# Float32 one-hots of the gate table laid out token by token

## The chip, the cores and the metric

The kernel runs on one core of a Trainium2 chip. The core has a matrix engine (TensorE, PE in the profile, with its weight loads shown apart as PEld), a vector engine (VectorE, DVE), a scalar engine (ScalarE, ACT), GpSimd (POOL) and a queue engine (SyncE, SP). They run side by side, each through its own list of instructions in order, and wait for each other by semaphores. The metric is the time of the program on the device in microseconds (us); smaller is better.

## The reference, cut to what matters

The program is one residual layer: two token mixers in parallel (RWKV-7 and S5), then PEER, a mixer over 128 x 128 = 16384 one-neuron experts, then a norm. What the change touches is PEER:

```python
sv, si = lax.top_k(s, PEER_TOPK)                       # 16 best of 128 keys, for both key halves
cv, ci = lax.top_k(cand.reshape(...), PEER_TOPK)       # 16 best of the 256 pairs
i1 = jnp.take_along_axis(si[:, :, 0], ci // PEER_TOPK, axis=-1)
i2 = jnp.take_along_axis(si[:, :, 1], ci % PEER_TOPK, axis=-1)
gate = jax.nn.softmax(cv, axis=-1)
hid = jax.nn.gelu(jnp.einsum('td,thkd->thk', xt, table_u[e]))    # e = i1 * 128 + i2
return jnp.einsum('thk,thkd->td', gate * hid, table_v[e])
```

Each of the 1024 tokens chooses 8 heads x 16 = 128 experts with a gate each. Everything is float32.

## The kernel before

The tokens stand in eight blocks of 128. Three blocks gather the rows of their experts from memory. The other five ("dense", 640 tokens) compute the scores of all 16384 experts with matmuls and weight them with a gate table that is zero wherever a token did not choose the expert. This table, `gd` in device memory, is made before the dense part by `gate_table`, one block of 128 tokens after the other.

For a token, the table is a 128 x 128 matrix, first key by second key. It is a product of two one-hot matrices with the 128 choices of the token on the partitions: `a` has a 1 at the second key of each choice, `b` has the gate at its first key. So a token needs one 128x128x128 float32 matmul `gm`, which the machine runs as two weight loads and two matmul instructions. The tokens go through in groups of four (TG = 4); 640 tokens are 160 groups and 1280 gm instructions. In a group:

- VectorE compares a constant `iotaM` with the keys, in bfloat16, for `aq` and for `bq` (in the profile `oaq` and `ohq`), all [128, 128 keys, 4 tokens], the four tokens innermost
- ScalarE (for a few groups VectorE) copies `aq` to float32 as `a` (`oha`)
- GpSimd, or VectorE where the planner found it free earlier, multiplies `bq` by the gates `gT` into float32 `b` (`ohb`)
- TensorE runs the four matmuls with `a[:, :, t]` as weights and `b[:, :, t]` as the moving side: 128 values that lie four floats (16 bytes) apart, since the tokens are interleaved
- ScalarE copies the four results from PSUM into `stg`, which holds 32 tokens, token innermost; so each token's 128 values are written 32 floats (128 bytes) apart. After eight groups a 2 MB transfer writes `stg` to `gd`

The buffers: three of `oha`, three of `ohb`, two of `ohq`, one of `oaq`, two PSUM banks of `gm`, two of `stg`.

The order of the instructions is not that of the code. A planner (class `Weave`) runs fourteen streams of the program as threads: the RWKV state, the top-k retrieval, the table, the gathers, the dense part and others. Each stream hands in operations; the planner holds estimated costs per engine (`cost`, by element counts alone, blind to strides), keeps a clock of every engine and of every buffer, and emits at each step the ready operation with the highest bonus on the engine that is free first. `nc.copy` and `nc.either` offer an operation to two engines, and it takes the one that would end first by its estimate. What it emits is then the fixed order of each engine. A buffer that is handed out again makes its next writer wait for the last reader. While the table is built, the last RWKV steps, the retrieval of the later blocks and, towards the end, the first dense scores `S` are woven between the groups. All operations go through one helper line, so the profile names them by tile. The dense stream with its gate loads `G` begins after the last table block.

Of the kernel before, what the change touches and what calls it, by code (L numbers as in the profile page):

```python
# [19 lines left out]
F32 = mybir.dt.float32  # L20
F32R = mybir.dt.float32r
BF = mybir.dt.bfloat16
# [3 lines left out]
OP = mybir.AluOpType  # L26
# [17 lines left out]
TG = 4  # L44
# [7 lines left out]
GW = 2  # L52
HG = 0
PB = 2
OA = 4
BV = 0
BDP = "none"
TREE = 1
# [316 lines left out]
class Kern:  # L375
# [1147 lines left out]
    def gate_table(self, blk, e, g, pool):  # L1523


        nc, v = self.nc, self.nc.vector
        p = self.ps("gp", [128, 3, 128], 1, self.psg)
        for i, src in enumerate((e[:, :, 0], e[:, :, 1], g)):
            x = pool.tile([128, 128], F32, name=self.nm("slc"), tag="slc", bufs=1)
            nc.copy(x.rearrange("p (h k) -> p h k", h=8), src)  # L1530
            nc.tensor.transpose(p[:, i], x, self.ident)
        iT = pool.tile([128, 2, 128], BF, name=self.nm("iT"), tag="iT", bufs=2)
        gT = pool.tile([128, 128], F32, name=self.nm("gT"), tag="gT", bufs=2)
        nc.copy(iT, p[:, 0:2])
        nc.copy(gT, p[:, 2])
        for t32 in range(4):
            stg = pool.tile([128, 128, 32], F32, name=self.nm("stg"), tag="stg", bufs=2)
            for t16 in range(32 // TG):
                t0 = 32 * t32 + TG * t16
                shp = [128, 128, TG]  # L1540
                bc = lambda x: x[:, None, t0:t0 + TG].to_broadcast(shp)
                a = pool.tile(shp, F32, name=self.nm("oha"), tag="oha", bufs=3)
                bq = pool.tile(shp, BF, name=self.nm("ohq"), tag="ohq", bufs=2)
                b = pool.tile(shp, F32, name=self.nm("ohb"), tag="ohb", bufs=3)
                if t16 % 4 < OA:
                    aq = pool.tile(shp, BF, name=self.nm("oaq"), tag="oaq", bufs=1)
                    v.tensor_tensor(aq, self.iotaM, bc(iT[:, 1]), op=OP.is_equal)
                    nc.copy(a, aq)
                else:
                    v.tensor_tensor(a, self.iotaM, bc(iT[:, 1]), op=OP.is_equal)  # L1550
                v.tensor_tensor(bq, self.iotaM, bc(iT[:, 0]), op=OP.is_equal)
                nc.either("tensor_tensor", b, bq, bc(gT), op=OP.mult)
                for t4 in range(TG // 4):
                    ps = self.ps("gm", [128, 4, 128], GMB, self.psg)
                    for i in range(4):
                        t = 4 * t4 + i
                        nc.tensor.matmul(ps[:, i], a[:, :, t], b[:, :, t], start=True, stop=True)
                    o = TG * t16 + 4 * t4
                    nc.copy(stg[:, :, o:o + 4].rearrange("p i t -> p t i"), ps)
            nc.sync.dma_start(self.gd[4 * DB.index(blk) + t32], stg)  # L1560
        self.tabled += 1
# [546 lines left out]
```

## Time and profile before

| | |
|---|---|
| time, median of 3 runs | 3720.68 us (3716.93 to 3731.84) |
| profiled execution, its own time | 3725.95 us |
| span in it, from first to last instruction | 3723.9 us |
| mean granted TensorE clock | 0.947 of full |
| busy: PE, PEld, DVE, ACT, POOL | 93%, 80%, 74%, 36%, 32% |
| the table stage, first to last `gm` | about 1274 to 1694 us |

Busy shares are means over a long program of unlike stages; what one stage is worth is read from rows of that stage. An instruction's duration counts from its start to its last result, so instructions that follow each other on one engine overlap: how fast an engine gets through them is read from the starts, or from the busy time of a stretch divided by the count.

### The profile page before, as it was taken

Reading aid. Unit: us, or ns where it says so; the run is one execution under the profiler, and the core shown is the slowest. Engines: PE = TensorE matmul, PEld = TensorE weight load, DVE = VectorE, ACT = ScalarE, POOL = GpSimd, SP = SyncE. Lnnn points to the kernel's source line nnn. Section 1 sums busy time; section 2 is a strip of 40 time slices with the busy share of each in tenths; the row PEclk is TensorE's granted clock in tenths of the full one; section 3 lists DMA queues with packets and bytes.
Section 4 is the critical chain, followed back from the end, with each engine's and each line's share of the span. In section 5 each row is a group of like instructions: output and inputs, shape, how many; then the busy total and the mean of one; then the engine's idle time right before and its main releaser. Section 6 shows DMA issues by size and latency. Waiting matters only on the chain.

```text
span 3723.9 us, 59743 instructions
## 1 busy us (share of the span) xinstructions
PE 3446.2 (93%) x22415; PEld 2975.6 (80%) x22415; DVE 2757.2 (74%) x6150; ACT 1346.6 (36%) x2905; POOL 1191.9 (32%) x1137
## 2 busy tenths in 40 slices
PE   7989999999888999998998889988999999999997
PEld 7777687767666888897787778887989998888986
DVE  7555413546999967654788978888888888888888
ACT  4332323333232466663233323333333333333333
POOL 3653323532443344432222222122222222222221
PEclk9998999998889899899999899998999999999998
DMA  5641223355577422257888799877898988898886
GB/s 205 215 152 54 88 96 119 129 195 187 168 260 236 166 100 92 98 191 255 312 318 317 246 327 334 304 269 276 304 323 303 323 316 308 306 322 290 304 298 228
DMA packets 359953, 869.11 MB, mean 233 GB/s; under 512 B 28960, under 2 KB 175520, under 8 KB 307952
## 3 DMA queue, kind: packets, MB, share of 16 engines
q1 hardware_dynamic: 303792, 461.01, 36.8%
q0 software_dynamic: 55296, 402.68, 29.4%
q8 instruction: 176, 2.88, 0.3%
q10 hardware_dynamic: 576, 1.61, 0.1%
q14 instruction: 113, 0.93, 0.1%
HBM read 759.16 MB, written 104.86 MB: 232 GB/s over the span
## 4 chain that ended last, share of the span: by engine, by line
PE 48%; DVE 19%; issue 15%; DMA 10%; POOL 5%; ACT 2%; SPq 1%; POOLq 0%; DVEq 0%; ACTq 0%
PE S L171 11%; PE acc L171 10%; PE gm L171 9%; PE mm L171 7%; POOL row L171 5%; DMA G<-gd 3%; PE tps L171 3%; PE rs L171 2%; PE gl L171 2%; PE rw L171 2%; DVE gacc L171 2%; PE pp L171 1%; DMA row<-in_uv_dram,ei 1%; DMA w<-in_wout_dram 1%; DVE ti L171 1%
## 5 line engine op out<-in xcount | busy, mean ns | idle before, releaser
L171 POOL DMA_INDIRECT row<-in_uv_dram,ei x384 | 519.0, 1352 | 1499.2 <-DVE gacc L171 1253.4
L171 PE MATMUL S<-dx,uh 128*128 128x320 f32 x4096 | 790.4, 314 | 8.5 <-ACT w L171 6.1
L171 PEld LDWEIGHTS S<-dx,uh 128*128 128x128 f32 x4096 | 656.9, 190 | 27.9 <-ACT w L171 9.5
L171 PE MATMUL acc<-vh,wh 128*128 128x512 f32 x1280 | 504.3, 402 | 64.1 <-DVE acc L171 61.7
L171 DVE SCALAR_TENSOR_TENSOR gacc<-row,hid,gacc 128x1024 f32<-128x1024 f32 x384 | 491.2, 1279 | 71.7 <-ACT hid L171 71.1
L171 PE MATMUL acc<-vl,wh 128*128 128x512 f32 x1280 | 511.2, 399 | 11.2 <-DVE vl L171 11.0
L171 PE MATMUL acc<-vh,wl 128*128 128x512 f32 x1280 | 509.4, 398 | 0.1
L171 PE MATMUL S<-dx,ul 128*128 128x320 f32 x2048 | 478.4, 314 | 13.0 <-DVE ul L171 13.0
L171 DVE CUSTOM_DVE_ANT_0 row<-row,gx 128x1024 f32<-128x1024 f32 x384 | 468.3, 1220 | 18.1 <-DMA row<-in_uv_dram,ei 18.0
L171 PEld LDWEIGHTS S<-dx,ul 128*128 128x128 f32 x2048 | 346.8, 190 | 17.9 <-DVE ul L171 15.9
L171 PE MATMUL gm<-ohb,oha 128*128 128x128 f32 x1280 | 343.1, 430 | 5.5 <-ACT oha L171 5.0
L171 PEld LDWEIGHTS acc<-vh,wh 128*128 128x128 f32 x1280 | 244.0, 191 | 128.0 <-DVE acc L171 67.2
L171 PEld LDWEIGHTS gm<-ohb,oha 128*128 128x128 f32 x1280 | 311.3, 329 | 14.3 <-ACT oha L171 5.1
L171 PEld LDWEIGHTS acc<-vl,wh 128*128 128x128 f32 x1280 | 246.2, 192 | 61.4 <-DVE vl L171 15.5
L171 PEld LDWEIGHTS acc<-vh,wl 128*128 128x128 f32 x1280 | 245.7, 192 | 54.7 <-issue 1.7
L171 ACT ACTIVATE hid<-hid 128x1 f32<-128x1 f32 x384 | 77.2, 201 | 564.2 <-DVE hid L171 563.3
L171 ACT ACTIVATE vh<-vr 128x512 fp32r<-128x512 f32 x256 | 160.3, 627 | 284.2 <-PE acc L171 166.3
L171 DVE TENSOR_TENSOR acc<-acc,acc 128x512 f32<-128x512 f32 x320 | 213.0, 682 | 6.9 <-PE acc L171 6.4
L171 ACT ACTIVATE stg<-gm 128x512 f32<-128x512 f32 x160 | 172.5, 1079 | 119.2 <-PE gm L171 116.5
L171 POOL TENSOR_TENSOR ohb<-ohq,gT 128x512 f32<-128x512 bf16 x135 | 146.0, 1082 | 212.8 <-DVE ohq L171 116.1
L171 DVE TENSOR_TENSOR vl<-vr,vh 128x512 fp32r<-128x512 f32 x255 | 174.3, 685 | 52.4 <-ACT vh L171 52.1
L171 DVE TENSOR_TENSOR w<-w,G 128x640 f32<-128x640 f32 x128 | 105.1, 821 | 144.7 <-DMA G<-gd 114.3
(443 smaller groups left out, 6241.8 us busy)
## 6 DMA issues: line engine op xcount, KB each, us to landing
ur<-in_ut_dram SPq DMA_DIRECT2D x128, 512.0 KB, 6.5
vr<-in_uv_dram SPq DMA_DIRECT2D x256, 256.0 KB, 6.4
wf<-wsd SPq DMA_DIRECT2D x120, 512.0 KB, 5.5
gd<-stg SPq DMA_DIRECT2D x20, 2048.0 KB, 6.6
G<-gd SPq DMA_DIRECT2D x31, 1280.0 KB, 16.6
wsd<-sw SPq DMA_DIRECT2D x40, 512.0 KB, 3.4
wr<-in_wc_dram SPq DMA_DIRECT2D x30, 512.0 KB, 4.7
wr<-in_wg_dram SPq DMA_DIRECT2D x32, 256.0 KB, 3.3
```

The lines of the kernel that those rows point to most:

```text
L171: op.alts = [(e, self.cost(e, n, outs, ins), lambda f=f, a=a, k=k: f(*a, **k)) for e, n, f, a, k in alts]
```

## The change

`a` and `b` become [128, 4 tokens, 128 keys], a token's 128 values side by side. The copy and the gate product write them through a turned view (`turn`), in the old order of elements, so that consecutive elements go to places 128 floats (512 bytes) apart. The matmuls read `a[:, t]` and `b[:, t]`, 128 adjacent floats. The comparisons and their results in bfloat16 stay as they were. `oaq` gets two buffers instead of one, and the branch on `OA`, which was always taken, goes.

```diff
-OA = 4
...
-                a = pool.tile(shp, F32, name=self.nm("oha"), tag="oha", bufs=3)
+                a, b = (pool.tile([128, TG, 128], F32, name=self.nm("oh" + x), tag="oh" + x, bufs=3) for x in "ab")
+                turn = lambda x: x.rearrange("p t m -> p m t")
                 bq = pool.tile(shp, BF, name=self.nm("ohq"), tag="ohq", bufs=2)
-                b = pool.tile(shp, F32, name=self.nm("ohb"), tag="ohb", bufs=3)
-                if t16 % 4 < OA:
-                    aq = pool.tile(shp, BF, name=self.nm("oaq"), tag="oaq", bufs=1)
-                    v.tensor_tensor(aq, self.iotaM, bc(iT[:, 1]), op=OP.is_equal)
-                    nc.copy(a, aq)
-                else:
-                    v.tensor_tensor(a, self.iotaM, bc(iT[:, 1]), op=OP.is_equal)
+                aq = pool.tile(shp, BF, name=self.nm("oaq"), tag="oaq", bufs=2)
+                v.tensor_tensor(aq, self.iotaM, bc(iT[:, 1]), op=OP.is_equal)
+                nc.copy(turn(a), aq)
                 v.tensor_tensor(bq, self.iotaM, bc(iT[:, 0]), op=OP.is_equal)
-                nc.either("tensor_tensor", b, bq, bc(gT), op=OP.mult)
+                nc.either("tensor_tensor", turn(b), bq, bc(gT), op=OP.mult)
...
-                        nc.tensor.matmul(ps[:, i], a[:, :, t], b[:, :, t], start=True, stop=True)
+                        nc.tensor.matmul(ps[:, i], a[:, t], b[:, t], start=True, stop=True)
```

The order of the instructions moves inside the table stage alone; ahead of it and behind it the engines' lists are as they were. The second buffer of `oaq` is what moves it: the planner's estimates do not see the strides. The count of copies on ScalarE goes from 156 to 158 of 160 (VectorE 4 to 2), and of gate products on GpSimd from 135 to 126 (VectorE 25 to 34).

ScalarE, near the start of the table stage, before. `stg` is a group's evacuation, `oha` a group's copy; the numbers of `gm` and `oha` grow with the groups, and the group of oha2654 is evacuated from gm2658, that of oha2659 from gm2664.

```order
L171 ACTIVATE oha2654_13897<-oaq2657_13905 128x512
L171 ACTIVATE stg2594_13714<-gm2653_13896 128x4x128
L171 ACTIVATE oha2659_13916<-oaq2662_13925 128x512
L171 ACTIVATE stg2594_13714<-gm2658_13915 128x4x128
L171 ACTIVATE oha2666_13936<-oaq2669_13946 128x512
L171 ACTIVATE Z2635_13839<-rx2637_13881 128x256
L171 ACTIVATE stg2594_13714<-gm2664_13934 128x4x128
```

The same place after the change; here the group of oha2660 is evacuated from gm2664.

```order
L170 ACTIVATE oha2660_13918<-oaq2663_13921 128x128x4
L170 ACTIVATE stg2594_13714<-gm2653_13893 128x4x128
L170 ACTIVATE oha2666_13937<-oaq2669_13940 128x128x4
L170 ACTIVATE stg2594_13714<-gm2658_13917 128x4x128
L170 ACTIVATE oha2672_13959<-oaq2675_13962 128x128x4
L170 ACTIVATE stg2594_13714<-gm2664_13935 128x4x128
```

Before, a copy stands one evacuation ahead of its own group's evacuation; after, two, so the copies run one group further ahead.

VectorE, some groups later, before. `ohq` and `oaq` are the two comparisons of a group, the rest is retrieval and RWKV work.

```order
L171 TENSOR_TENSOR ohq_13983<-iotaM,iT_13712 128x512
L171 MAX tv_13122<-t_13921 128x8
L171 TENSOR_TENSOR oaq_13991<-iotaM,iT_13712 128x512
L171 MAX_INDEX ti_13123<-tv_13122,t_13921 128x8
L171 MAX tv_13120<-sc_13611 128x8
L171 TENSOR_TENSOR ohq_14005<-iotaM,iT_13712 128x512
L171 MAX_INDEX ti_13121<-tv_13120,sc_13611 128x8
L171 TENSOR_TENSOR oaq_14015<-iotaM,iT_13712 128x512
```

The same place after the change.

```order
L170 TENSOR_TENSOR oaq_13980<-iotaM,iT_13712 128x512
L170 TENSOR_TENSOR ohq_13979<-iotaM,iT_13712 128x512
L170 MAX_INDEX ti_13123<-tv_13122,sc_13553 128x8
L170 MATCH_REPLACE t_13912<-tv_13122,sc_13553 128x128
L170 TENSOR_TENSOR abm_13991<-pb_12577,cst 128x256
L170 TENSOR_TENSOR oaq_14008<-iotaM,iT_13712 128x512
L170 TENSOR_TENSOR ohq_14007<-iotaM,iT_13712 128x512
```

The two comparisons of a group now stand together, `oaq` first, with the other work behind the pair and not between.

## Rows read from the trace of the kernel before

**Rows 1.** The page: span, and busy time of each engine

```profile
span 3723.9 us, 59743 instructions
PE 3446.2 (93%) x22415; PEld 2975.6 (80%) x22415; DVE 2757.2 (74%) x6150; ACT 1346.6 (36%) x2905; POOL 1191.9 (32%) x1137
```

**Rows 2.** Windows: busy us (instructions) by engine, granted clock, DMA share, GB/s

```profile
core 0: us, PE busy (x) PEld busy (x) DVE busy (x) ACT busy (x) POOL busy (x), PEclk, DMA share, GB/s
1274.00:1694.00 420.00, 406.11 (x2405) 372.73 (x2405) 272.64 (x741) 270.51 (x412) 182.77 (x161) 0.92 0.31 117
1280.00:1580.00 300.00, 291.06 (x1890) 259.99 (x1889) 211.66 (x612) 189.26 (x302) 135.40 (x121) 0.91 0.23 95
1580.00:1694.00 114.00, 109.31 (x491) 107.59 (x491) 54.98 (x116) 77.41 (x105) 43.80 (x38) 0.96 0.52 179
1720.00:1760.00 40.00, 27.66 (x140) 23.41 (x141) 23.86 (x35) 8.21 (x20) 5.22 (x4) 0.83 0.76 264
```

**Rows 3.** Windows of the evacuation `stg` alone: ScalarE's busy us (count)

```profile
1280.00:1580.00 300.00, 117.30 (x111) 0.91 0.23 95
1580.00:1694.00 114.00, 52.07 (x49) 0.96 0.52 179
```

**Rows 4.** The chain of waits: start us, us, what

```profile
1586.85 23.66 PE gm L171 x96
1610.51 0.11 PE gp L171
...
1693.88 1.15 ACT stg L171
1695.04 7.66 DMA gd<-stg
1702.76 8.27 DMA G<-gd
```

**Rows 5.** Instructions on `gm`: duration ns min/median/max, first and last start

```profile
L171 PEld LDWEIGHTS gm<-ohb,oha x1280: 307/332/335, 1274.0 to 1693.2; 128*128 128x128 f32 x183
L171 PE MATMUL gm<-ohb,oha x1280: 388/416/604, 1274.0 to 1693.4; 128*128 128x128 f32 x183
```

**Rows 6.** The same view of RWKV's float32 128x128 matmuls with adjacent values

```profile
L171 PEld LDWEIGHTS rm<-lo,lora x192: 186/191/337, 386.7 to 1416.8; 128*128 128x128 f32 x192
L171 PE MATMUL rm<-lo,lora x192: 270/275/422, 386.7 to 1416.9; 128*128 128x128 f32 x192
```

**Rows 7.** Groups of instructions of the table stage: busy us, mean ns, idle before

```profile
L171 PE MATMUL gm<-ohb,oha 128*128 128x128 f32 x1280 | 343.1, 430 | 5.5 <-ACT oha L171 5.0 <-issue 0.5
L171 ACT ACTIVATE stg<-gm 128x512 f32<-128x512 f32 x160 | 172.5, 1079 | 119.2 <-PE gm L171 116.5 <-DMA gd<-stg 2.5
L171 POOL TENSOR_TENSOR ohb<-ohq,gT 128x512 f32<-128x512 bf16 x134 | 145.0, 1082 | 200.1 <-DVE ohq L171 116.1 <-PE gm L171 51.2 <-DVE rtrg L171 10.5
L171 ACT ACTIVATE oha<-oaq 128x512 f32<-128x512 bf16 x155 | 98.2, 633 | 15.8 <-DVE oaq L171 15.8
L171 DVE TENSOR_TENSOR oaq<-iotaM,iT 128x512 bf16<-128x512 bf16 x159 | 93.1, 585 | 121.3 <-ACT oha L171 112.7 <-ACT iT L171 7.9
L171 DVE TENSOR_TENSOR ohb<-ohq,gT 128x512 f32<-128x512 bf16 x25 | 18.2, 727 | 4.2 <-PE gm L171 3.5
```

**Rows 8.** Groups of whole program: PSUM copies to adjacent places, and one to places apart

```profile
L171 ACT ACTIVATE sc<-tp 128x512 f32<-128x512 f32 x24 | 14.3, 597 | 25.2 <-PE tp L171 25.2
L171 DVE TENSOR_TENSOR h<-mm,h 128x512 f32<-128x512 f32 x12 | 8.1, 685 | 6.6 <-PE mm L171 6.6
L171 DVE COPY yT<-tps 128x512 f32<-128x512 f32 x8 | 8.6, 1152 | 17.5 <-PE tps L171 17.5
```

**Rows 9.** Timeline of ScalarE: start us, us, instruction, idle before

```profile
1448.36 1.04 ACT L171 ACTIVATE stg<-gm 128x512 f32<-128x512 f32 x1 [1.21 <-PE gm L171]
1449.20 0.63 ACT L171 ACTIVATE oha<-oaq 128x512 f32<-128x512 bf16 x1
```

## The prediction, made before the changed kernel had run

> **What bounds the kernel now.** I read the page first: PE is busy 93% of a span of 3723.9 us [rows 1], so where a stage has PE waiting for nothing, time spent by PE is time of the program. Then the windows around the only instructions that the change alters, the table stage from 1274 to 1694 us: PE is busy 406.1 of 420 us, VectorE 272.6, ScalarE 270.5, GpSimd 182.8 [rows 2]. So this stage is TensorE's. Third, the groups: the gm matmuls take 343.1 us of PE and were kept waiting 5.5 us, while ScalarE's evacuation `stg` waited 116.5 us for gm, and VectorE's `oaq` 112.7 us for the copy `oha` that frees its single buffer [rows 7]: the other engines queue up behind gm. Last, the chain of waits: it runs through gm, once through 96 of them without a break, and from the last evacuation over the last write of `gd` straight into the first gate load of the dense part [rows 4]. What the stage loses in length, the program loses, since behind it the instructions and their order are the same.
>
> **What the change removes.** In the unbroken run 96 instructions take 23.66 us, 246 ns each [rows 4]. Their neighbour `gp`, a float32 128x128 instruction on adjacent values, takes 0.11 us of the chain [rows 4]. The durations say the same: gm's loads and matmuls have medians of 332 and 416 ns, the adjacent `rm` of the same shape 191 and 275 [rows 5, 6], 141 ns less on either side. With gm at 110 ns, PE is relieved of 1280 x 136 ns = 174 us, and its 406 us in the stage become 232. Its bound there is gone, and what is late next decides.
>
> A rule of the Trainium skill bears on this: "SBUF — State Buffer", section "Door 1: The DMA port swizzle", holds that 4 float32 values is as far as one can stride for free, since a line has 16 bytes. By that figure the interleaved reads would cost nothing and the change would leave the time at 3721. The rows differ: the loads at that stride take 332 against 191 ns [rows 5, 6]. The measurement decides.
>
> **What it adds.** The writers now step 512 bytes from element to element. The trace has no such write, but two with steps: `stg` writes 128 bytes apart and takes 1079 ns, where a ScalarE copy from PSUM of the same size to adjacent places takes 597 [rows 7, 8]; VectorE's `yT`, 32 bytes apart, takes 1152, where a VectorE operation from PSUM to adjacent places takes 685 [rows 8]. So a stepped float32 write costs 470 to 480 ns more on both engines, about twice the time per element. From this:
>
> ScalarE: 158 copies x 0.48 = +76 us. The bounds of this price are 0 (if a copy from SBUF hides it) and about twice 0.48 (if 512 bytes are worse than 128); I take 0.48, the value of the row nearest in engine and size.
>
> VectorE: 34 products at 727 + 470 = 1197 ns are 40.7 us against 18.2 before, +22 us; the two copies that leave it give back 1. Bounds 0 and +45.
>
> GpSimd: no stepped write of it is in the trace. Its product takes 1082 ns for 512 elements [rows 7], slower than the stepped write of either other engine by element minus its fixed part, so the step may vanish in it. Bounds: 0, and three times its duration. I take between 0 and 0.5 us each, at most 126 x 1.58 = 199 us in place of 145, and GpSimd at 183 + 54 = 237 us: off the path either way.
>
> The second `oaq` buffer takes away VectorE's wait for the copy of the group just before; the wait for the one before that stays, and the copies stand one group further ahead in ScalarE's list. This hides under PE before and matters only now, since ScalarE's evacuation no longer finds gm unfinished.
>
> **The sum.** By groups: the first part, with RWKV and retrieval woven in, has 111 groups in 300 us, 2.70 us each; the second 49 in 114, 2.33 us each [rows 2, 3]. In the first part ScalarE needs 189.3/111 = 1.71 us per group now, and 1.71 + 0.47 = 2.18 after. That counts records that start behind idle time. Where its list is full, the next one starts 0.84 us after a `stg` of 1.04 [rows 9], so a full list would get through the two stepped writes in 1.7 and some 0.2 of the rest, 1.9. VectorE needs 211.7/111 = 1.91 us, and 2.04 after. PE needs 2.62 - 8 x 0.136 = 1.53. ScalarE and VectorE are then equals at about 2.0 to 2.1, they wait for each other, and PE before reached 97% alone; I take 2.2 us per group. In the second part VectorE has little else (55.0/49 = 1.12), ScalarE needs 1.58 + 0.47 = 2.05, or 1.9 with a full list: I take 2.0. So 111 x 0.50 + 49 x 0.33 = 56 + 16 = 72 us less. The stage would take about 348 us. The changes of block, where index transposes, copies and comparisons must run through before the next gm, cost a few us each and stay.
>
> Against the profiled execution's own time of 3725.95 (2 us over its span) that is 3654. The median of the runs lies 5.3 us lower at 3720.68, which gives **3649**.
>
> **Rivals.**
>
> *The stepped copy is free on ScalarE.* For it: its source is SBUF and half as wide, unlike `stg`'s. Against: VectorE and ScalarE pay the same in the two rows there are, which points to the write. Then VectorE binds in the first part at about 2.1 and ScalarE in the second at 1.65: 111 x 0.60 + 49 x 0.68 = 100 us less, 3621.
>
> *The gain is eaten.* If the copy's step costs twice `stg`'s (+0.95 us), ScalarE needs 1.71 + 0.94 = 2.65 us in the first part and 2.5 in the second, with overlap perhaps 0.2 less: the stage stays within 20 us of 420, the time at 3705 to 3735, say 3718. For it: 512 bytes is four times as far; against: 32 and 128 bytes cost the same.
>
> *TensorE's clock falls.* In the stage the granted clock is 0.92 with PE busy 97%; behind it, where PE is busy 27.7 of 40 us (69%), it is 0.83 [rows 2], a mix of the levels 1.2 and 2.4 GHz. After the change PE would have 232 of 348 us, 67%, so a clock near 0.83 is likely, and 232 x 0.92/0.83 = 257 us still fits. At the lower level throughout, an adjacent matmul needs up to 422 - 275 = 147 ns more [rows 6], 1280 x 0.257 = 329 us with gm alone, 392 with the other 63 as they are: the stage would shrink by some 27 us and the time be 3694. The Trainium skill, "TensorE: Matmul & The Clock Gate", section "A second HAM failure mode: psum-queue depth-cycling", describes this kind of stage: short idle times between groups make the clock fall back again and again. The 0.83 of rows 2 agrees in kind.
>
> *GpSimd's stepped product is slow.* If it handles such writes one by one at 4 us a product, 126 x 4.0 + 38 of other work = 542 us, and the stage takes 120 us longer: 3843. It decides from (420 - 38)/126 = 3.0 us a product, three times today's duration, at which all its work fills the old stage. Nothing in the trace excludes it, but neither engine that shows such writes pays more than twice.
>
> *The stride is not what makes gm slow.* Then nothing changes on PE: 3721. Rows 5 and 6 have the same shape and type and differ in the stride alone, so this is small.
>
> **Chances.** Forecast 0.60 (3620 to 3680 is its own range); free copy 0.14; gain eaten 0.09; clock 0.07; GpSimd 0.06; stride not the cause 0.04. About 0.5%, 19 us, is what a measurement of this kernel can tell from no change. Faster by more: the forecast, the free copy, most of the clock case and a little of the eaten gain, 0.82. Within: most of the eaten gain, stride and a rest of the others, 0.11. Slower: GpSimd and a piece of the eaten gain, 0.07. The range 3605 to 3705 takes in the free copy with some room and the clock case, and leaves GpSimd and the eaten gain out.
>
> **What would show it.** gm's loads near 190 ns and matmuls near 275. `oha` on ScalarE near 1.1 us; if it is 0.63, the first rival. `ohb` on GpSimd below 1.6 us; if over 3, the fourth. The stage from first to last gm near 350 us, with PE at about two thirds, ScalarE at over 90%, and `stg` no longer waiting for gm but ScalarE waited for by gm and `oaq`. Behind the stage the lengths should be as before to within some us; if the dense part grows by what the stage loses, the argument that the stage's length passes through is wrong.

## The result, and the profile after

The change makes the kernel faster: 3671.61 us (median of 4 runs, 3657.96 to 3678.38) against 3722.39 of the kernel before in the same comparison, a ratio of 0.9851 with a 95% interval of 0.9824 to 0.9878. Run again later beside other kernels it gave 3669.61 us and 0.9864 (0.9824 to 0.9905). That is 50 to 55 us. The forecast was 3649, 72 less than before, with a range of 3605 to 3705: the direction holds and TensorE's bound is gone as argued; the size was set too high.

The profiled execution has a span of 3666.8 us, 57.1 less. The page first: TensorE's busy share fell, though the kernel got faster, and that of VectorE and ScalarE rose; rows 1 had 93%, 74% and 36%.

```profile
span 3666.8 us, 59750 instructions
PE 3317.5 (90%) x22415; PEld 2841.2 (77%) x22415; DVE 2807.3 (77%) x6159; ACT 1398.3 (38%) x2906; POOL 1205.8 (33%) x1127
```

The instructions on `gm` and its makers after the change (duration in ns, minimum, median, maximum; first and last start). They answer to rows 5: gm's load and matmul now have the durations of the adjacent `rm` of rows 6, and the last gm starts at 1631 instead of 1693. The stepped copy takes 1122 ns, the stepped product 1120 on GpSimd and 1068 on VectorE (medians).

```profile
L170 PEld LDWEIGHTS gm<-ohb,oha x1280: 186/192/338, 1274.9 to 1631.1; 128*128 128x128 f32 x183
L170 PE MATMUL gm<-ohb,oha x1280: 272/275/582, 1274.9 to 1631.2; 128*128 128x128 f32 x183
...
L170 ACT ACTIVATE oha<-oaq x158: 1066/1122/1362, 1272.6 to 1627.9; 128x512 f32<-128x512 bf16 x158
...
L170 POOL TENSOR_TENSOR ohb<-ohq,gT x126: 1070/1120/3270, 1272.9 to 1626.8; 128x512 f32<-128x512 bf16 x126
L170 DVE TENSOR_TENSOR ohb<-ohq,gT x34: 1001/1068/3177, 1344.0 to 1624.9; 128x512 f32<-128x512 bf16 x34
```

The windows of the table stage, from the first gm to the last, in the columns of rows 2. Before, PE was busy 97% of the stage; now it is 75%, and VectorE and ScalarE stand side by side at 89%. The second and third line are the two parts of the stage that the prediction's sum goes by.

```profile
1274.00:1632.00 358.00, 267.84 (x2360) 229.83 (x2361) 320.32 (x750) 319.15 (x411) 185.06 (x152) 0.89 0.35 133
...
1280.00:1550.00 270.00, 206.09 (x1965) 175.63 (x1965) 258.29 (x629) 242.20 (x319) 151.09 (x124) 0.90 0.28 114
1550.00:1632.00 82.00, 56.66 (x362) 49.67 (x361) 56.03 (x107) 71.63 (x84) 29.64 (x25) 0.88 0.62 207
```

The waits of the stage after (who waited for whom: us in total, times, longest). `stg` waited 116.5 us for gm before [rows 7] and now 16.0; the direction has turned, and gm waits for `stg` to free its bank.

```profile
POOL ohb L170 <- DVE ohq L170: 101.7, 81, 3.4
PE gm L170 <- ACT stg L170: 38.2, 71, 1.7
...
DVE oaq L170 <- ACT oha L170: 18.6, 23, 4.7
ACT stg L170 <- PE gm L170: 16.0, 12, 6.0
```

And the chain of waits, which ran through gm before [rows 4], now goes by turns over ScalarE and VectorE: of the stage's length ScalarE's two stepped writes have 35% on it, VectorE's two comparisons 21%, gm 5%. Where ScalarE's list is full, its writes follow each other every 0.90 us:

```profile
1448.70 0.92 ACT stg L170
1449.62 0.90 ACT oha L170
1450.52 0.91 ACT stg L170
1451.44 0.90 ACT oha L170
```

Where the 57 us of the span come from, by the first starts of gm and of the dense part's `acc`: up to the first gm +0.9; first to last gm 419.4 to 356.3, -63.1; last gm to first acc 19.4 to 29.2, +9.8; from there to the end 2011 to 2006, -4.7.

The +9.8 is work that stood between the groups and now stands behind them. Until the first `acc` both kernels run the same 192 score instructions `S`. Here are those behind the last gm (PE, PEld, DVE, ACT, POOL): before, after, and from two kernels of the experiments, the kernel before with a second buffer of `oaq` and the change with one buffer:

```profile
1693.00:1713.00 20.00, 16.57 (x107) 15.83 (x107) 0.00 (x0) 1.87 (x6) 0.00 (x0) 1.00 0.91 295
1631.00:1661.00 30.00, 25.22 (x163) 23.92 (x163) 0.00 (x0) 2.30 (x6) 0.00 (x0) 1.00 0.76 254
1692.00:1723.00 31.00, 26.77 (x163) 25.49 (x163) 0.00 (x0) 2.30 (x7) 0.00 (x0) 0.94 0.77 260
1667.00:1687.00 20.00, 16.46 (x107) 15.70 (x107) 0.00 (x0) 2.27 (x6) 0.00 (x0) 1.00 0.94 304
```

107 of the 192 came behind the last gm before, 163 after: 56 more, and 8.7 us more of PE, on the path. The number goes with the planner's order and not with the layout: the old layout with a second buffer has 163, too, and 30.7 us to the first acc, and the new layout with one buffer has 107 and 19.2 us. So the second buffer moved these 56 instructions out of the stage, and the stage looks shorter by them. So TensorE's list behind the last gm is not as it was, other than stated with the change.

### The profile page after: what moved, and what is told of

It reads as the page before. It is cut to its first block, busy times and chain, and to the rows that moved or that the text cites. A ratio compares the mean times of both kernels' runs of the same rounds, so it can differ in the third digit from the quotient of the medians.

```text
span 3666.8 us, 59750 instructions
## 1 busy us (share of the span) xinstructions
PE 3317.5 (90%) x22415; PEld 2841.2 (77%) x22415; DVE 2807.3 (77%) x6159; ACT 1398.3 (38%) x2906; POOL 1205.8 (33%) x1127
## 4 chain that ended last, share of the span: by engine, by line
PE 37%; DVE 25%; issue 16%; DMA 9%; ACT 6%; POOL 6%; SPq 1%; POOLq 0%; DVEq 0%; ACTq 0%
PE S L170 10%; PE acc L170 10%; PE mm L170 7%; POOL row L170 5%; PE tps L170 3%; DMA G<-gd 2%; DVE gacc L170 2%; DMA vr<-in_uv_dram 2%; ACT stg L170 2%; ACT oha L170 2%; PE rs L170 2%; PE gl L170 2%; DVE row L170 1%; PE pp L170 1%; PE rw L170 1%
## 5 line engine op out<-in xcount | busy, mean ns | idle before, releaser
L170 DVE SCALAR_TENSOR_TENSOR gacc<-row,hid,gacc 128x1024 f32<-128x1024 f32 x384 | 491.5, 1280 | 63.8 <-ACT hid L170 63.3
L170 PE MATMUL gm<-ohb,oha 128*128 128x128 f32 x1280 | 200.4, 308 | 57.3 <-ACT stg L170 38.2
L170 PEld LDWEIGHTS gm<-ohb,oha 128*128 128x128 f32 x1280 | 174.8, 213 | 75.7 <-issue 35.1
L170 PE MATMUL mm<-xnH,wh 128*128 128x512 f32 x480 | 196.3, 409 | 6.2 <-DVE pm L170 6.2
L170 PE MATMUL mm<-xnH,wl 128*128 128x512 f32 x480 | 194.7, 406 | 0.7 <-POOL wl L170 0.7
```

What stands on the lines that cost most here:

```text
L170: op.alts = [(e, self.cost(e, n, outs, ins), lambda f=f, a=a, k=k: f(*a, **k)) for e, n, f, a, k in alts]
```

## The experiments

The stage alone does not compare kernels well, since `S` may fall inside it or behind it. So the table has the stretch from the first start of gm to the first start of acc as well, which holds the same 192 instructions `S` in all of them. The two lengths (us) come from one profiled execution of each kernel, the times are medians of 4 to 10 runs, and each ratio is to runs of the kernel before taken beside them.

| kernel | first to last gm | first gm to first acc | time, median | ratio to before, 95% |
|---|---|---|---|---|
| before | 419.4 | 438.8 | 3722 to 3725 | 1 |
| the change | 356.3 | 385.5 | 3671.6 | 0.985 (0.982 to 0.988) |
| weights adjacent alone | 391.6 | 422.3 | 3711.9 | 0.996 (0.994 to 0.998) |
| moving side adjacent alone | 397.3 | 428.0 | 3713.4 | 0.996 (0.995 to 0.998) |
| second buffer alone | 407.2 | 437.9 | 3723.1 | 1.000 (0.998 to 1.002) |
| layout with one buffer | 382.9 | 402.1 | 3684.8 | 0.989 (0.986 to 0.992) |
| plain copy | 342.7 | 372.0 | 3658.0 | 0.985 (0.982 to 0.989) |
| plain product | 349.0 | 380.7 | 3673.6 | 0.989 (0.985 to 0.992) |
| both plain | 332.1 | 361.3 | 3652.4 | 0.983 (0.979 to 0.986) |
| comparisons adjacent | 415.5 | 446.0 | 3735.9 | 1.004 (1.002 to 1.006) |
| products on VectorE | 383.3 | 448.1 | 3723.4 | 1.000 (0.998 to 1.002) |
| products on GpSimd | 360.2 | 379.4 | 3656.8 | 0.981 (0.978 to 0.984) |
| the change again | 354.9 | 385.6 | 3669.6 | 0.986 (0.982 to 0.991) |

**One side of the matmul at a time.** In the first kernel `b` stays interleaved, in the second `a`:

```diff
-                nc.either("tensor_tensor", turn(b), bq, bc(gT), op=OP.mult)
+                nc.either("tensor_tensor", old(b), bq, bc(gT), op=OP.mult)   # old: the view [128, 128, 4] of the tile
...
-                        nc.tensor.matmul(ps[:, i], a[:, t], b[:, t], start=True, stop=True)
+                        nc.tensor.matmul(ps[:, i], a[:, t], old(b)[:, :, t], start=True, stop=True)
```

> Changed kernel, but b stays interleaved: only the weights a are adjacent, and only the copy on ScalarE steps. Theory (a weight load runs beside the matmul ahead of it, so the pitch of gm is the slower of the two): the matmul stays at about 416 ns, the load falls to 191, the pitch stays near 246 ns, PE keeps its 400 us in the table stage and the time is that of before, 3710 to 3735 us, oha at 1.1 us having bought nothing. Rival (both sides add to the pitch): pitch near 178 ns, PE near 320 us in the stage, time 3675 to 3695 us.

> Changed kernel, but a stays interleaved: only the moving side b is adjacent, only the product steps, and the copy on ScalarE is plain at 0.63 us. Theory (the pitch is the slower of load and matmul): load 332 ns, matmul 275, pitch near 246, time 3710 to 3730 us. Rival (both sides add): pitch near 178, and with a cheap copy the stage is bound at about 2.05 us a group, 3640 to 3670 us, faster than the change.

With adjacent weights alone, the load falls to 208 ns and the matmul stays at 405; with the moving side adjacent alone, 329 and 397. The 275 ns expected for that last matmul did not come. Its duration stays long beside a slow load, so the 416 ns of rows 5 alone do not show that the moving read was slow; the first kernel shows it, where the load is fast and the matmuls come no closer. From one start to the next, the matmuls of gm are 236 ns apart before (median), 227 in the first kernel, 233 in the second and 112 after the change. The windows of gm alone:

```profile
1279.20:1670.80 391.60, 316.29 (x1279) 254.56 (x1280) 173.20 (x159) 0.94 0.32 122
```

```profile
1277.70:1675.00 397.30, 325.10 (x1280) 306.72 (x1280) 171.83 (x159) 0.95 0.32 120
```

316 and 325 us over 1280 instructions are 247 and 254 ns each, against 268 before [rows 7] and 157 after the change (busy time, with gaps and stretches at the lower clock in it). So the slower of load and matmul all but sets the pitch, and nearly all of the gain needs both sides. Both times lie in the ranges expected, near their lower ends. That the two kernels still gain 0.4% is of a size with the 21 and 12 us that gm's busy time fell against the 337 us that it has with the second buffer alone, the kernel with their order and the old layout; why it fell by that is not shown. The paid stepped copy did not make the first slower than before: while PE binds, ScalarE's extra 60 us are hidden.

**The order apart from the layout.** The kernel before with two buffers of `oaq`, and the change with one:

```diff
-                    aq = pool.tile(shp, BF, name=self.nm("oaq"), tag="oaq", bufs=1)
+                    aq = pool.tile(shp, BF, name=self.nm("oaq"), tag="oaq", bufs=2)
```

> Kernel before with two buffers of oaq and nothing else: the order of the change without its layout. Theory (PE binds the stage, so when copies may start is worth nothing): 3715 to 3730 us, gm still 246 ns apart. Rival (a part of the gain comes from the buffer and the order): 3690 to 3710 us.

> Changed kernel with one buffer of oaq: the layout with the order of before. Theory (behind the change ScalarE and VectorE bind together, and one buffer makes each comparison wait for the copy of the group before, now 1.1 us long): a part of the gain is lost, stage 375 to 400 us, time 3685 to 3710 us, with VectorE waiting for oha more than 60 us. Rival (the buffer plays no part, the layout is all): 3660 to 3680 us.

The buffer alone is worth nothing (1.000), and with the layout about 13 to 15 us, with ratios whose intervals overlap a little: without it 3684.8, 0.2 below the range expected. VectorE then waits 65.0 us for `oha` in place of 18.6. A buffer that costs nothing under one bound is worth something under the next. This also settles whether the gain is the layout's or the order's: mostly the layout's. By the stretch to acc the order alone saves 0.9 us, the layout alone 36.7, the two together 53.3.

**The price of the stepped writes.** The same order of instructions, with copy or product or both written to adjacent places. These kernels leave out the step, and the matmuls, which read as in the change, then make another table than the reference's:

```diff
-                nc.copy(turn(a), aq)
+                nc.copy(old(a), aq)
...
-                nc.either("tensor_tensor", turn(b), bq, bc(gT), op=OP.mult)
+                nc.either("tensor_tensor", old(b), bq, bc(gT), op=OP.mult)
```

> Changed kernel whose copy writes oha to adjacent places in the old interleaved order, while the matmuls read it as token rows: the table's values are then not the reference's; what is left out is the stepping of ScalarE's write alone. The order of instructions is that of the change. Theory (behind the change ScalarE and VectorE, 319 and 320 of 358 us, bind the stage together): oha falls to 0.63 us, ScalarE to about 250 us, but VectorE stays near 310 to 320, so the stage ends at 335 to 345 us and the time at 3650 to 3662. Rival (ScalarE binds alone): stage near 300, time 3605 to 3625.

> Changed kernel whose gate product writes ohb to adjacent places in the old interleaved order, the matmuls reading it as token rows: values not the reference's; left out is the stepping of the product's write alone. Theory: GpSimd's product hardly changes (1.12 to 1.04 us), VectorE gains 34 x 0.38 = 13 us, ScalarE stays at 319, the stage at 345 to 356 us, time 3660 to 3672. Rival (GpSimd's stepped write slows VectorE's operations through what the two share): oaq falls below 0.55 us on average, VectorE to 285 or less, time 3640 to 3655.

> Changed kernel with both writes to adjacent places in the old order (values not the reference's; both stepped writes left out): the matmuls' gain without the writers' price. Theory (the writers' price is what keeps the change from the whole gain): ScalarE 250, VectorE 300, PE 265 us, stage 320 to 335 us, time 3635 to 3650, so that the price of the steps is 20 to 40 us of the program. Rival (the stage is held by chains of waits and not by busy time): 3660 to 3672.

With the plain copy, ScalarE falls to 265 us of a stage of 343, and the stage shortens by 14 us only; the chain of waits goes over to VectorE, whose two comparisons have 43% of it. The window of this kernel and that of the kernel with both plain:

```profile
1273.90:1616.60 342.70, 266.81 (x2354) 228.08 (x2355) 325.44 (x750) 265.49 (x408) 176.64 (x151) 0.88 0.37 139
```

```profile
1279.60:1611.70 332.10, 261.99 (x2355) 223.45 (x2355) 317.47 (x750) 262.92 (x408) 173.22 (x151) 0.89 0.38 144
```

VectorE is busy 95 and 96%. So behind TensorE two engines stand close together, and taking the load off one of them shows the other. The steps cost 17 to 19 us of time together (3652 against 3670 and 3672, with intervals that overlap a little), just under the 20 to 40 expected, with a time 2 us above its range; the writers' price is not the larger part of what is left. The plain product alone shortened the stretch to acc by 5 us and not the time (3673.6, 1.6 above its range), which is within the noise. Neither engine binds alone, as the theory had it, but VectorE's 317 us in the last kernel are above the 300 that the theory gave it.

**The same layout without stepped writes.** The comparisons work token by token, too:

```diff
-                shp = [128, 128, TG]
-                bc = lambda x: x[:, None, t0:t0 + TG].to_broadcast(shp)
+                shp = [128, TG, 128]
+                bc = lambda x: x[:, t0:t0 + TG, None].to_broadcast(shp)
```

> Another way to the same layout, with the reference's values: iotaM, oaq and ohq stand token by token too, the comparisons read the key of a token as a broadcast along the innermost 128, and copy and product write adjacent places; nothing steps. If the comparisons keep their 0.42 us: as both plain, 3635 to 3650 us. Rival (a comparison with an innermost broadcast loses the faster rate and takes 0.6 us or more): VectorE at 350 to 385 us binds the stage, 3690 to 3720 us, slower than the change.

The rival's mechanism came true, and its price was more than it said: a comparison takes 685 ns (`oaq`, median) instead of 421 where the key is the same over the innermost 128, and VectorE's 401 us, not 350 to 385, bind a stage of 416. At 3736 us, over the range of 3690 to 3720, it is 0.4% slower than before. So the interleaved order is worth keeping for the comparisons, with four different keys side by side.

**What stretches VectorE.** All products on one engine:

```diff
-                nc.either("tensor_tensor", turn(b), bq, bc(gT), op=OP.mult)
+                v.tensor_tensor(turn(b), bq, bc(gT), op=OP.mult)        # in the other kernel: nc.gpsimd.tensor_tensor
```

> Changed kernel with all 160 gate products on VectorE (stepped, 1.07 us each), none on GpSimd. It tests what stretches VectorE's operations. Theory (an operation of VectorE with two operands in SBUF stands still while GpSimd's product runs): oaq and ohq fall to 0.40 to 0.45 us on average (from 0.63 and 0.52), abm from 1.08 to about 0.45; VectorE then has some 171 us of products, 135 of comparisons and 85 of the rest, 390 us, and the stage takes 400 to 420 us, time 3705 to 3730. Rival (the stretch comes from ScalarE's or VectorE's own stepped writes): oaq and ohq stay at 0.5 us or more, stage over 430, time over 3735.

> Changed kernel with all 160 gate products on GpSimd. VectorE loses 39 us of products and gains some 12 of standing still, GpSimd rises to about 225 us. Theory (ScalarE and VectorE bind together): VectorE at 290 to 295 us, ScalarE alone binds at 318 of some 345 us, stage 340 to 350, time 3652 to 3666, a little faster than the change. Rival (the products were moved to VectorE where GpSimd was late, so its queue becomes the wait): stage 360 us or more, time 3672 or more.

> The changed kernel itself once more, on the same chip as the two others: 3660 to 3680 us, stage 352 to 360 us.

Without products on GpSimd, VectorE's comparisons are short; with all of them there, long. The groups of the three kernels (count, busy us, mean ns): on VectorE, the change, on GpSimd.

```profile
L170 DVE TENSOR_TENSOR oaq<-iotaM,iT 128x512 bf16<-128x512 bf16 x160 | 69.6, 435 | 22.4 <-ACT oha L170 7.3 <-ACT iT L170 4.8
L170 DVE TENSOR_TENSOR ohq<-iotaM,iT 128x512 bf16<-128x512 bf16 x160 | 69.4, 434 | 0.0
```

```profile
L170 DVE TENSOR_TENSOR oaq<-iotaM,iT 128x512 bf16<-128x512 bf16 x160 | 100.9, 631 | 23.0 <-ACT oha L170 18.6 <-ACT iT L170 4.1
L170 DVE TENSOR_TENSOR ohq<-iotaM,iT 128x512 bf16<-128x512 bf16 x160 | 83.3, 521 | 1.0 <-POOL ohb L170 1.0
```

```profile
L170 DVE TENSOR_TENSOR oaq<-iotaM,iT 128x512 bf16<-128x512 bf16 x160 | 111.2, 695 | 17.7 <-ACT oha L170 16.9 <-ACT iT L170 0.4
L170 DVE TENSOR_TENSOR ohq<-iotaM,iT 128x512 bf16<-128x512 bf16 x160 | 94.5, 591 | 4.6 <-POOL ohb L170 4.6
```

The timelines show single cases. Before, an `oaq` starts inside GpSimd's product and ends 0.28 us behind its end (first pair). After the change VectorE's `abm`, 0.41 us on average in the stage before, does the same and ends 0.17 us behind it; `MATCH_REPLACE8` ahead of it, which reads one 128x128 operand and the eight values of `tv`, keeps its 0.27 us inside the same product:

```profile
1446.99 1.06 POOL L171 TENSOR_TENSOR ohb<-ohq,gT 128x512 f32<-128x512 bf16 x1 [3.00 <-DVE ohq L171]
1447.27 1.06 DVE L171 TENSOR_TENSOR oaq<-iotaM,iT 128x512 bf16<-128x512 bf16 x1
...
1288.09 1.17 POOL L170 TENSOR_TENSOR ohb<-ohq,gT 128x512 f32<-128x512 bf16 x1 [1.57 <-DVE ohq L170]
...
1288.27 0.27 DVE L170 MATCH_REPLACE8 t<-tv,sc 128x128 f32<-128x128 f32 x1
1288.46 0.97 DVE L170 TENSOR_TENSOR abm<-pb,cst 128x256 f32<-128x256 f32 x1
```

They are the rule. Of the 329 `oaq`, `ohq` and `abm` on VectorE in the stage before, 51 take over 0.6 us; each of the 51 met a two-operand operation of GpSimd, running already or started less than 0.15 us after it, and ended 0.28 us behind that one's end (0.278 to 0.285). After the change they are 91, and 90 of them end 0.12 to 0.29 us behind such an operation; with the products on VectorE 10 are left. So in these VectorE stands still until GpSimd is through. Not every overlap draws one out: 55 before and 56 after overlap such an operation and take 0.6 us or less, in part because VectorE's had started first. What the long ones take beyond 0.42 us adds up to 32.7 us before, 32.0 with the second buffer alone, 48.1 with the layout and one buffer, 56.3 after the change and 75.2 with all products on GpSimd.

The Trainium skill, "GPSIMD Engine Reference", section "8. Key points", says that GpSimd shares its SBUF interfaces with VectorE and that VectorE's instructions with two SBUF inputs contend with it; the trace agrees, with means of 411 ns for the nine `abm` in the stage before and 1083 after.

The kernel with products on VectorE is no faster than before (3723.4). `oaq` and `ohq` came out as the theory had it; that the time fell in its range is luck. The stage took 383 us and not 400 to 420, with VectorE at 353 and not 390, but the order that the planner then made left all 192 `S` and their loads behind the table, 65 us from the last gm to the first acc.

With all products on GpSimd the time is 3656.8 us, 13 to 15 less than the change in either of its runs, with a ratio of 0.9812 (0.9782 to 0.9842): the fastest kernel here with the reference's values. Its interval overlaps those of the change, so that it beats the change is likely and not settled. Its stage was expected to shrink and did not (360.2): VectorE stayed at 317 us where 290 to 295 were expected, with 19 us more of standing still and not 12. What it gains lies behind the stage, where the planner left 106 `S` and not 163: 19 us from the last gm to acc and not 29 to 31. That makes 6.2 of the 6.6 us between its profiled span and that of the change again; the medians lie 13 apart, and the rest is not shown. So the theory of this kernel had the time right and the stage wrong, and the rival the reverse.

## Why the prediction came out as it did

*TensorE bound the stage by its reads at a 16-byte step, and both of its reads:* right. 332 and 416 ns became 192 and 275, and it takes both sides. Sized too high: the sum took 174 us off PE and gave it 232 in the stage, and it is 268. gm's own busy time fell from 343 to 200 us; its matmuls came 124 ns closer (236 to 112), not 136, and not all of them. Where the granted clock was at the lower of its two levels they stand 213 ns apart (182 distances inside groups), where the stepped reads had kept them 236 ns apart at either level (135 at the lower). 1280 x 124 ns less 182 x 101 ns are 140 us, of the 143 measured. With the order of before PE would stand at 280 (the layout with one buffer); it binds in neither order.

*The stepped copy on ScalarE, +0.48 us:* right; 1122 ns against 633 is +0.49, and `stg`'s row was the right neighbour. As a total, +76 us overstated it: ScalarE's busy time rose by 47, since in a full list the records overlap. The lower bound from the overlap, 0.84 us per write, came close to the measured 0.90.

*VectorE:* the step that was mis-sized. The prediction added 21 us for stepped products and came to 294; measured are 319. The products themselves came out at 38.7 us for the 40.7 set down (mean 1139 ns, with standing still in it; the median is 1068, a step of +377 ns and not +470). What is missing is 26 us, most of it standing still behind GpSimd's operations: the long comparisons and `abm` went from 51 to 91, and what they take beyond 0.42 us grew by 24 us. In means, `oaq` went from 584 to 631 ns, `ohq` from 463 to 521, `abm` from 411 to 1083. The second buffer alone adds nothing to that sum (32 us), the layout alone 15, so it comes with the shorter stage. The trace of before had it in view, `oaq` with a mean of 585 [rows 7] beside a median of 426; the prediction took that mean as a property of the operation and let it stay as it was.

*GpSimd's stepped product:* 1120 against 1041 ns, in the lower part of its bounds, off the path as said. That GpSimd was slower by element than the stepped writes of the others, from which the prediction argued, is in no row: 1082 ns stand against 1079 and 1152. The step itself slows VectorE little if at all: with the plain product `oaq` and `ohq` have means of 605 and 511.

*The groups:* 2.2 and 2.0 us were forecast. 119 groups in 270 us and 40 in 82 are 2.27 and 2.05, so the stage took 356 us and not 348. That 2.2 came so close is in part luck: in the first part VectorE needed 258.3/119 = 2.17 us per group where 2.04 had been set down, and ScalarE 242.2/119 = 2.04 where the sum had 2.18, or 1.9 with a full list.

*What the stage loses, the program loses:* not quite, and this is the other step that failed. The dense part is about as long as before (-4.7), but 56 score instructions that had stood between the groups came behind the last one, +9.8 us. The prediction held that the instructions behind the stage and their order are the same. The second buffer had moved these 56 in the planner's order, and the kernel with that buffer alone has 30.7 us behind its last gm. This and the 9 us by which the stage fell short make the miss of 15 us in the profiled execution (57 against 72), less some 4 by which the rest was shorter.

*The rivals:* the free copy and the eaten gain are excluded by 1122 ns; the slow GpSimd by 1120. The clock fell from 0.92 to 0.89 in the stage, not to 0.83, and PE at 75% had room for it; at the lower level a matmul took 213 ns and not the 257 that the rival set down. That the stride was not the cause is excluded by rows 5 against the rows above.

## What to carry to other kernels

Look at what a matmul reads in both of its operands: here a step of 16 bytes in float32 doubled the pitch (236 against 112 ns), and making one of the two adjacent gained almost nothing, since the slower side sets it. A layout change moves the price to the writers: here a stepped write of 512 float32 took 0.49 us more on ScalarE, 0.38 in VectorE's product and 0.08 on GpSimd. It pays while the writers have slack, so sum up the engines that come next, not only the one relieved. Where a mean lies far above its median, look in the timeline for what the long ones wait for: here it was GpSimd, and it grew when the stage was compressed. And a change that also moves the planner's order may shift work over the edge of the stage by which it is measured.

## What was not expected of the hardware

With its operands 16 bytes apart gm keeps 236 ns from start to start at either level of the granted clock; with adjacent ones it has 112 and 213. A bfloat16 comparison of 512 elements takes 421 ns with four different keys innermost and 685 with one key broadcast over the innermost 128. VectorE's copy from SBUF with a step takes 712 ns (two of them) against 428 (four), less of a rise than the 467 between the two rows from PSUM [rows 8], which are of two different operations. The 51 two-operand operations of VectorE that one of GpSimd draws out before the change all end 0.28 us after that one's end. With one side adjacent, gm's busy time still falls by 4 to 6%, though the other side is about as slow as before (405 and 329 ns); why stays open.
